# Where a sparse layer's first query projections stand, how memory attention is interleaved, and a final norm taken per token

## The chip, the cores and the metric

The kernel is one program on one core of a Trainium2 chip. The metric is the device time of the whole program in microseconds (us). TensorE (PE) does the matrix products and PEld its weight loads, VectorE is DVE, ScalarE is ACT, GpSimd is POOL, and SyncE (SP) issues most of the DMAs.

## What is computed

The reference is a trunk of two layers over 512 tokens of 1024 features. Each layer adds a mixer and then a gated convolutional FFN to `h`; at the end `h` is normalised. Cut to its frame:

```python
for i in range(DEPTH):                      # DEPTH = 2
    if i == 1:
        shared = shared_kv(h, ...)          # keys and values of the sparse layer
    xn = rmsnorm(h, norm_mix[i])
    mem_kv = rmsnorm(mem, norm_mem[i]) @ w_mem_kv[i]      # 256 memory rows, 4 heads of 64
    if i == 0:                              # gated linear attention
        q, k, v, g, lr, mq = split_cols(xn @ gla_w_in[i], GLA_SIZES)
        main = gla_mixer(...)
    else:                                   # sparse attention, 12 heads of 64, 4 groups
        q, gl, mq = split_cols(xn @ nsa_w_in[0], NSA_SIZES)
        main = nsa_mixer(q, sigmoid(gl), shared, rel_bias)
    mo = mem_attention(mq, mem_kv)          # softmax(mq mem_k) mem_v
    h = h + concatenate([main, mo], -1) @ w_out[i]
    h = h + conv_ffn(rmsnorm(h, norm_ffn[i]), ...)
return rmsnorm(h, final_norm)               # x * rsqrt(mean(x*x) + eps) * gain, per token
```

In `nsa_mixer` every head attends to 31 compressed keys, to selected blocks and to a window, each with a bias by distance.

## The kernel before

**Layout.** Activations stand transposed: `h[k]` (k = 0 to 7) holds 128 features of all 512 tokens. For products in near fp32, `split` makes two fp32r tiles of each: a high half by an ACT copy and the rest by a DVE subtraction (`xh`, `xl`, or `Qh`, `Ql`). A projection onto 128 columns (`projA`) is 8 x 3 = 24 matmuls of 512 columns: wh with xh, wl with xh, wh with xl. `stepsB` makes the values, whose result stands with tokens on the partitions: for each k and each of four token tiles again three matmuls.

**Weights.** `wget` fetches 512 KB by an SP DMA into `wraw` (three buffers), in layer 1 scales it by the gain on POOL, and splits it: ACT makes `wh`, DVE makes `wl`. PSUM has four tags of two banks: `acc`, `sc`, `pt` and `po`.

**Norms.** The squares of `h` are added up into `sqacc` (ACT squares, DVE adds, `sq_step`). `rms_finish` takes the sums over features with four matmuls against a column of ones (L303), makes the reciprocal roots with a POOL `pow` (L306), puts them on a diagonal (DVE, L310), spreads them over the partitions with one matmul of 512 columns (L312) and copies the result to `rb` (ACT).

**Order.** A scheduler sets the order on each engine from the order in which the code is written and from its own estimate of when operands come. In the sparse layer `mm` and `tr` chain TensorE's instructions, so that they stay in written order.

- The start (`gla_layer`): the split of the input, 24 small matmuls for the low-rank gate (`wlr`), then six query and key projections, with `rms_finish` after the first has begun.
- Memory attention (`mem_att`, both layers): twice, for a pair of heads each, it copies the queries to both halves of the partitions (`dup`, four DMAs on SP), splits them, and goes through four tiles of 128 tokens: scores (L395), softmax on DVE and ACT, transposes of the weights (L409), and `fill()`, which emits some steps of the values. At the end of each pair it multiplies the values with the transposed weights (L417).
- Layer 1 after memory attention: `project(0)` (the query projection of the first sparse head pair), `queries(0)` (its `dup` and split, and the `strip` DMAs of the biases), half of `project(1)`, `compressed(0)`, the other half, and `scores(0)`. Then a loop of twelve steps, in which scores, transposes, values and later projections alternate.
- The end (`build`): `rms_finish`, eight products of `h` and the gain on ACT (L1095), eight with `rb` on DVE and POOL (L1098, L1100), and eight DMAs of 256 KB to `outT`, which the host transposes.

## Time and profile before

| | before |
|---|---|
| device time, three runs | 1352.37, 1353.55, 1356.32 us (median 1353.55) |
| the profiled execution | 1353.9 us, with a span of 1352.1 us |
| granted TensorE clock, mean | 0.986 |
| TensorE busy | 1302.7 us, 96% of the span |
| VectorE, ScalarE, GpSimd busy | 840.7, 590.9, 123.3 us |
| DMA | 129.95 MB, 96 GB/s |

The profile is one execution. The span is what it recorded; the 1.8 us by which the execution's own time is longer lies outside. A matmul of 512 columns counts as 0.39 us busy, but the next starts while it drains, so two stand 0.23 us apart at the full clock. An fp32 matmul leaves two records, so counts of those are twice the program's. The granted clock is given as a share of full speed, where 1.00 is 2.4 GHz and 0.50 is 1.2 GHz; a mean between them is a mixture of the two.

### The profile page before, as it was taken

What the parts mean: (1) busy time and instruction counts of PE and PEld (TensorE: products, weight loads), DVE (VectorE), ACT (ScalarE), POOL (GpSimd) and SP (SyncE); (2) the same over time, 40 slices, a digit from 0 to 9 for tenths busy, and PEclk for the clock granted to TensorE, in tenths of its full rate; (3) what the DMA queues carried; (4) which work ended last, traced back from release to release, by engine and by line L of the source; (5) the groups of instructions that cost most, each with busy time, mean ns of one, the idle gap of its engine ahead of it and who ended that gap; (6) DMA issues with size and microseconds to landing.
All of it is one profiled execution on the core that took longest, in us unless ns stands there. A gap on an engine that the chain in (4) does not pass through costs nothing.

```text
span 1352.1 us, 17979 instructions
## 1 busy us (share of the span) xinstructions
PE 1302.7 (96%) x6868; PEld 1052.5 (78%) x6868; DVE 840.7 (62%) x1374; ACT 590.9 (44%) x1060; POOL 123.3 (9%) x102
## 2 busy tenths in 40 slices
PE   7999998999999999999999988999999999999995
PEld 4887776878888888887787666778888888888884
DVE  7556777577777774334466577675577777773223
ACT  6446554444444443223234465665344444442222
POOL 1000000000000000002124243442000000000001
PEclk9999998999999999999999989999999999999997
DMA  6342110323333333333565333211233333333321
GB/s 228 108 136 78 32 33 31 112 81 95 100 101 94 94 97 103 97 94 114 135 186 150 113 88 95 75 47 33 94 94 95 95 102 99 94 94 98 103 65 62
DMA packets 43577, 129.95 MB, mean 96 GB/s; under 512 B 5783, under 2 KB 10039, under 8 KB 43492
## 3 DMA queue, kind: packets, MB, share of 16 engines
q1 hardware_dynamic: 41504, 125.91, 31.6%
q10 hardware_dynamic: 1988, 2.89, 0.7%
q8 instruction: 54, 0.88, 0.3%
q14 instruction: 31, 0.25, 0.1%
HBM read 116.16 MB, written 2.15 MB: 87 GB/s over the span
## 4 chain that ended last, share of the span: by engine, by line
PE 90%; DVE 4%; ACT 2%; DMA 1%; issue 1%; POOL 1%; SPq 0%; DVEq 0%; ACTq 0%; POOLq 0%
PE acc L265 39%; PE acc L709 18%; PE acc L656 6%; PE sc L892 3%; PE po L892 3%; PE acc L284 2%; PE acc L515 2%; PE po L284 2%; PE pt L893 2%; PE acc L892 2%; PE acc L796 2%; PE pt L573 1%; PE sc L824 1%; PE sc L265 1%; PE sc L656 1%
## 5 line engine op out<-in xcount | busy, mean ns | idle before, releaser
L233 DVE TENSOR_TENSOR wl<-wraw,wh 128x1024 fp32r<-128x1024 f32 x196 | 246.6, 1258 | 163.6 <-ACT wh L232 161.3
L232 ACT ACTIVATE wh<-wraw 128x1024 fp32r<-128x1024 f32 x196 | 207.6, 1060 | 290.6 <-PE acc L709 105.9
L265 PE MATMUL acc<-xh,wh 128*128 128x512 f32 x800 | 313.5, 392 | 0.5 <-ACT wh L232 0.5
L265 PE MATMUL acc<-xh,wl 128*128 128x512 f32 x800 | 312.2, 390 | 0.8 <-DVE wl L233 0.8
L265 PE MATMUL acc<-xl,wh 128*128 128x512 f32 x800 | 312.7, 391 | 0.0
L265 PEld LDWEIGHTS acc<-xh,wh 128*128 128x128 f32 x800 | 150.5, 188 | 34.5 <-ACT wh L232 1.9
L265 PEld LDWEIGHTS acc<-xh,wl 128*128 128x128 f32 x800 | 150.6, 188 | 32.6 <-DVE wl L233 1.1
L265 PEld LDWEIGHTS acc<-xl,wh 128*128 128x128 f32 x800 | 150.6, 188 | 31.8 <-issue 0.5
L709 PE MATMUL acc<-ah,wh 128*128 128x512 f32 x352 | 136.9, 389 | 0.0
L709 PE MATMUL acc<-ah,wl 128*128 128x512 f32 x352 | 136.9, 389 | 0.0
L709 PE MATMUL acc<-al,wh 128*128 128x512 f32 x352 | 136.9, 389 | 0.0
L690 DVE TENSOR_TENSOR u<-acc,rb 128x512 f32<-128x512 f32 x88 | 60.6, 688 | 71.2 <-PE acc L265 69.7
L229 POOL TENSOR_TENSOR wraw<-wraw,vec 128x1024 f32<-128x1024 f32 x20 | 38.4, 1925 | 444.9 <-DMA wraw<-in_wp 438.4
L246 ACT ACTIVATE ah<-hc 128x512 fp32r<-128x512 f32 x44 | 27.8, 632 | 116.0 <-DVE hc L697 116.0
L709 PEld LDWEIGHTS acc<-ah,wl 128*128 128x128 f32 x352 | 66.1, 188 | 13.8
L709 PEld LDWEIGHTS acc<-ah,wh 128*128 128x128 f32 x352 | 66.1, 188 | 13.7
L709 PEld LDWEIGHTS acc<-al,wh 128*128 128x128 f32 x352 | 66.1, 188 | 13.7
L692 ACT ACTIVATE hc<-u,vec 128x512 f32<-128x512 f32 x88 | 71.1, 808 | 2.3 <-DVE u L690 1.6
L993 POOL TENSOR_TENSOR P<-P,ssm 128x256 f32<-128x256 f32 (+3 forms) x48 | 62.4, 1321 | 72.3 <-DVE ssm L990 41.1
L693 DVE SCALAR_TENSOR_TENSOR hc<-u,vec,hc 128x511 f32<-128x511 f32 x88 | 65.6, 745 | 5.2 <-ACT hc L692 5.2
L694 DVE SCALAR_TENSOR_TENSOR hc<-u,vec,hc 128x510 f32<-128x510 f32 x88 | 66.1, 751 | 3.1
L696 ACT ACTIVATE hc<-hc 128x512 f32<-128x512 f32 x44 | 27.8, 633 | 83.2 <-DVE hc L694 83.2
(310 smaller groups left out, 2050.0 us busy)
## 6 DMA issues: line engine op xcount, KB each, us to landing
wraw<-in_wp SPq DMA_DIRECT2D x200, 512.0 KB, 3.7
strip<-vecd SPq DMA_DIRECT2D x12, 448.0 KB, 3.6
qd<-qf SPq DMA_DIRECT2D x40, 128.0 KB, 2.3
mt<-in_memT SPq DMA_DIRECT2D x16, 128.0 KB, 3.0
kd<-kf SPq DMA_DIRECT2D x16, 128.0 KB, 2.4
h<-in_xT SPq DMA_DIRECT2D x4, 256.0 KB, 6.4
h<-in_xT ACTq DMA_DIRECT2D x4, 256.0 KB, 6.4
mkd<-mkf SPq DMA_DIRECT2D x16, 64.0 KB, 2.0
```

Of the source, the lines that this page charges most:

```text
L232: nc.scalar.activation(wh, raw, AF.Copy)
L233: nc.vector.tensor_tensor(out=wl, in0=raw, in1=wh.bitcast(F32), op=ALU.subtract)
L265: self.nc.tensor.matmul(ps[:M, :N], a[:, ws], b[:, :N], start=n == 0, stop=n == 23)
L284: nc.tensor.matmul(ps[:, :N], s_, m_, start=k == 0 and n == 0, stop=k == KC - 1 and n == 2)
L656: nc.tensor.matmul(banks[m], a[:, o], b, start=k == 6 and i == 0, stop=k == 5 and i == 2)
L690: nc.vector.tensor_tensor(out=u, in0=ps, in1=rb, op=ALU.mult)
L692: nc.scalar.activation(c, u, AF.Identity, scale=tap(2), bias=tap(3))
L693: nc.vector.scalar_tensor_tensor(out=c[:, 1:], in0=u[:, :S - 1], scalar=tap(1), in1=c[:, 1:], op0=ALU.mult, op1=ALU.add)
L694: nc.vector.scalar_tensor_tensor(out=c[:, 2:], in0=u[:, :S - 2], scalar=tap(0), in1=c[:, 2:], op0=ALU.mult, op1=ALU.add)
L709: nc.tensor.matmul(ps, a[:, o], x, start=n == 0, stop=n == 3 * NJ - 1)
L892: mm = lambda *args, **kw: pe(nc.tensor.matmul(*args, **kw))
L993: nc.gpsimd.tensor_tensor(out=P, in0=P, in1=f[:, i, :].unsqueeze(2).to_broadcast([128, 2, 128 * t + 128]), op=ALU.mult)
```

## The change

There are four parts.

- **Start.** Fourteen fp32 128 x 128 products of a tile of ones stand first on TensorE (their result is not used). The first three weights are split ahead of the squares, and their three projections stand ahead of `rms_finish`. The first takes its eight `wl` products last.
- **Memory attention.** One routine goes through both pairs of heads. Each tile's transposes are issued after the next tile's scores, and the first pair's values product after the second pair's first scores. The values product alternates between the halves of the partitions. `stepsB` yields after each three matmuls, `fill` emits 6 (layer 0) or 4 (layer 1) such steps, and `first` emits 8 steps ahead of the first scores.
- **Sparse layer.** The helpers `project`, `queries`, `pe`, `mm` and `tr` move ahead of memory attention without change but for the pool that they allocate from. `project(0)` becomes what `first` emits; `queries(0)`, the values, and then `project(1)` are the filling. After memory attention come `compressed(0)` and `scores(0)` alone.
- **End.** `last_residual` takes the place of the last norm. The output is written with tokens on the partitions, so the scale of a token is one number per partition.

```diff
+        idle = self.ps("pt")
+        for _ in range(14):
+            nc.tensor.matmul(idle[:, :128], self.ones, self.ones, start=True, stop=True)
...
+        steps = [(k, u, i) for k in range(KC) for u, i in ((wh, 0), (wl, 0), (wh, 1))]
+        if late:
+            steps.sort(key=lambda t: t[1] is wl)
...
         Q[0] = self.stack_q(qfs[0], pool)
+        first()
+        for m in range(2):
+            for qt in range(4):
+                scores(m, qt)
+                if m and not qt:
+                    out(0)
+                if qt == 3 and not m:
+                    Q[1] = self.stack_q(qfs[1], pool)
+                if qt:
+                    turn(m, qt - 1)
+                fill()
+            turn(m, 3)
             fill()
...
+        out(1)
...
+                ps = self.ps("po")
+                self.projA(ps, w, M=16)
+                early = [self.wget(self.W[name][j]) for j, name in ((0, "glak"), (0, "glaq"), (1, "glak"))]
                 for k in range(KC):
                     self.sq_step(k, self.h[k], S)
-                ps = self.ps("po")
-                self.projA(ps, w, M=16)
...
+                qps = [self.ps(tag) for tag in ("acc", "acc", "sc")]
+                for i in range(3):
+                    self.projA(qps[i], early[i], late=i == 0)
                 rc, rb = self.rms_finish(S, "")
...
+                def others():
+
+                    gen = project(0)
+                    for _ in range(8):
+                        yield run(gen, 3)
+                    q = queries(0)
+                    run(q)
+                    for i, _ in enumerate(values()):
+                        if i == 16:
+                            run(q, 3)
+                        yield
+                    gen = project(1)
+                    for _ in range(8):
+                        yield run(gen, 3)
+
+                vs = others()
+                upto = lambda n: lambda: run(vs, n)
+                self.mem_att(qfs, mp, mK, mV, mo, upto(8), upto(4))
...
-                run(project(0), 24)
-                q, c = queries(0), compressed(0)
-                run(q)
-                proj = project(1)
-                run(proj, 12)
-                run(q, 4)
+                c = compressed(0)
                 run(c)
-                run(proj, 12)
                 first = scores(0)
```

The new end, with the old one behind it:

```diff
+    def last_residual(self, m, ps):
+
+        nc, h = self.nc, self.h[m]
+        if m < 7:
+            nc.vector.tensor_tensor(out=h, in0=ps, in1=h, op=ALU.add)
+            self.sq_step(m, h, S)
+            self.hg.append(self.t(self.xp, [128, S], "xh"))
+            nc.scalar.activation(self.hg[m], h, AF.Copy, scale=self.gain(7, m))
+            return
+        sq = self.t(self.tmp, [128, S], "sq", bufs=2)
+        for c in range(2):
+            cs = slice(256 * c, 256 * c + 256)
+            nc.vector.tensor_tensor(out=h[:, cs], in0=ps[:, cs], in1=h[:, cs], op=ALU.add)
+            nc.scalar.activation(sq[:, cs], h[:, cs], AF.Square)
+        self.hg.append(self.t(self.xp, [128, S], "xh"))
+        nc.vector.tensor_scalar_mul(self.hg[m], h, self.gain(7, m))
+        sums = self.ps("pt")
...
+                nc.tensor.transpose(turned[t, half][:, 128 * (k % 4):128 * (k % 4) + 128], self.hg[k][:, tile(t)], self.ident)
+
+        for t in range(4):
+            nc.tensor.matmul(sums[:, t:t + 1], self.sqacc[:, tile(t)], self.ones[:, 0:1], start=True, stop=False)
+            nc.tensor.matmul(sums[:, t:t + 1], sq[:, tile(t)], self.ones[:, 0:1], start=False, stop=True)
+        for t in range(4):
+            turn(t, 0, range(4))
+        rc = self.t(self.small, [128, 4], "rc", bufs=2)
+        nc.vector.tensor_scalar(rc, sums[:, :4], 1.0 / D, EPS, op0=ALU.mult, op1=ALU.add)
+        nc.gpsimd.tensor_tensor(out=rc, in0=rc, in1=self.mhalf[:, :4], op=ALU.pow)
+        for t in range(4):
+            turn(t, 1, (4, 5, 6, 7))
+        for t in range(4):
+            y = self.t(self.wraw, [128, D], "wraw") if t < 3 else self.t(self.wsp, [128, D], "wh")
+            nc.scalar.activation(y[:, :512], turned[t, 0], AF.Copy, scale=rc[:, t:t + 1])
+            nc.vector.tensor_scalar_mul(y[:, 512:], turned[t, 1], rc[:, t:t + 1])
+            nc.sync.dma_start(self.out[128 * t:128 * t + 128, :], y)
...
-            rb = self.rms_finish(S, "")[1]
-            for k in range(KC):
-                nc.scalar.activation(hg[k], self.h[k], AF.Copy, scale=self.gain(7, k))
-            for k in range(KC):
-                if k % 3 == 2:
-                    nc.gpsimd.tensor_tensor(out=hg[k], in0=hg[k], in1=rb, op=ALU.mult)
-                else:
-                    nc.vector.tensor_tensor(out=hg[k], in0=hg[k], in1=rb, op=ALU.mult)
-                (nc.scalar if k % 2 else nc.sync).dma_start(self.out[128 * k:128 * k + 128, :], hg[k])
```

Two places show how TensorE's order moves, and a third SP's. The first is TensorE at the start of layer 1's memory attention. Before, the last product of the second memory query projection (L265) stands directly ahead of the first scores (L395):

```order
L265 MATMUL acc_5934<-xl_5148,wh_5930 128x512
L395 MATMUL sc_5977<-mK_1082_5770,Qh_1114_5964 128x256
L395 MATMUL sc_5977<-mK_1082_5770,Ql_1115_5965 128x256
L284 MATMUL acc_5999<-wh_6006,xh_4508 128x512
L284 MATMUL acc_5999<-wl_6007,xh_4508 128x512
```

Now the 24 products of `project(0)` (L946, the last two of them here) stand there, and the second head's scores (`mK_1085`, `Qh_1118`, `Ql_1119`) one and six rows behind the first head's:

```order
L946 MATMUL acc_6000<-xh_5162,wl_5997 128x512
L946 MATMUL acc_6000<-xl_5163,wh_5996 128x512
L397 MATMUL sc_6027<-mK_1083_5788,Qh_1115_5982 128x256
L397 MATMUL sc_6027<-mK_1083_5788,Ql_1116_5983 128x256
L285 MATMUL acc_6049<-wh_6056,xh_4523 128x512
L397 MATMUL sc_6027<-mK_1085_5794,Qh_1118_5989 128x256
L285 MATMUL acc_6049<-wl_6057,xh_4523 128x512
L285 MATMUL acc_6049<-wh_6056,xl_4524 128x512
L285 MATMUL acc_6050<-wh_6056,xh_4523 128x512
L285 MATMUL acc_6050<-wl_6057,xh_4523 128x512
L397 MATMUL sc_6027<-mK_1085_5794,Ql_1119_5990 128x256
```

Before, the second head's first scores stood 20 rows behind the first head's (a step of 12 values products and other scores between them).

The second place is TensorE from the compressed scores (`kcT`) of `compressed(0)` to the scores of `scores(0)` (`sc` from `K` and `Q`). Before, half of `project(1)` (twelve products into `acc_6376`, of which the first and the last stand here) lay between them:

```order
L892 MATMUL sc_6399<-kcT_5178,qf_6359 128x31
L892 MATMUL sc_6400<-kcT_5178,qf_6359 128x31
L892 MATMUL acc_6376<-xh_4874,wh_6372 128x512
...
L892 MATMUL acc_6376<-xl_5148,wh_6372 128x512
L892 MATMUL sc_6434<-K_951_5173,Qh_1212_6389 128x256
L892 MATMUL sc_6434<-K_951_5173,Ql_1213_6390 128x256
L892 MATMUL sc_6443<-K_951_5173,Qh_1212_6389 128x512
```

Now the scores follow directly, behind the values product of memory attention's second pair (L425):

```order
L425 MATMUL pt_6412<-mPT_1188_6282,mV_5842 64x512
L946 MATMUL sc_6431<-kcT_5193,qf_6025 128x31
L946 MATMUL sc_6432<-kcT_5193,qf_6025 128x31
...
L946 MATMUL sc_6452<-K_952_5188,Qh_1173_6215 128x256
L946 MATMUL sc_6452<-K_952_5188,Ql_1174_6216 128x256
L946 MATMUL sc_6461<-K_952_5188,Qh_1173_6215 128x512
L946 MATMUL sc_6461<-K_952_5188,Ql_1174_6216 128x512
```

From there to the first transposes of the sparse weights, TensorE has the same products in both kernels, but none of `project(1)` now.

The third place is SP's queue around the memory queries' copies (`qd` from `qf`). Before:

```order
L218 DMA wraw_6251<-in_wp 128x1024
L327 DMA qd_5961<-qf_5925 64x512 x2
L218 DMA wraw_6327<-in_wp 128x1024
L327 DMA qd_5968<-qf_5925 64x512 x2
L218 DMA wraw_6369<-in_wp 128x1024
```

Now two bias strips have come between the copies, and one ahead of them:

```order
L974 DMA strip_6047<-vecd_2703 128x896
...
L221 DMA wraw_6205<-in_wp 128x1024
L328 DMA qd_5979<-qf_5943 64x512 x2
L974 DMA strip_6219<-vecd_2703 128x896
L221 DMA wraw_6291<-in_wp 128x1024
L974 DMA strip_6520<-vecd_2703 128x896
L328 DMA qd_5986<-qf_5943 64x512 x2
```

## Rows read from the trace of the kernel before

**Rows 1.** The page: busy time of TensorE, and the chain that ended last

```profile
PE 1302.7 (96%) x6868; PEld 1052.5 (78%) x6868; DVE 840.7 (62%) x1374; ACT 590.9 (44%) x1060; POOL 123.3 (9%) x102
...
PE 90%; DVE 4%; ACT 2%; DMA 1%; issue 1%; POOL 1%; SPq 0%; DVEq 0%; ACTq 0%; POOLq 0%
```

**Rows 2.** Busy time by stretch; behind it clock, DMA share, GB/s

```profile
75.00:115.00 40.00, 39.93 (x208) 31.47 (x206) 20.99 (x38) 20.15 (x43) 0.00 (x0) 1.00 0.39 111
...
726.00:752.00 26.00, 23.42 (x103) 16.78 (x103) 17.95 (x29) 12.58 (x29) 7.69 (x5) 0.93 0.39 109
...
780.00:792.00 12.00, 7.98 (x26) 5.07 (x25) 9.29 (x33) 8.51 (x24) 3.97 (x4) 0.72 0.38 98
792.00:920.00 128.00, 117.70 (x986) 93.78 (x986) 93.97 (x297) 82.19 (x238) 55.47 (x46) 0.99 0.24 66
...
1334.00:1352.20 18.20, 3.10 (x10) 1.47 (x10) 7.79 (x10) 5.84 (x10) 4.44 (x3) 0.60 0.31 115
```

**Rows 3.** Timeline of the start: start us, duration, instruction [idle before]

```profile
10.82 1.41 DVE L250 SCALAR_TENSOR_TENSOR xl<-h,vec,xh 128x512 fp32r<-128x512 f32 x2
...
13.96 0.51 PE L265 MATMUL acc<-xh,wh 128*128 128x512 f32 x1 [0.51 <-ACT wh L232]
...
15.22 0.50 PE L265 MATMUL acc<-xh,wl 128*128 128x512 f32 x1 [0.75 <-DVE wl L233]
...
22.06 1.05 PE L303 MATMUL pt<-ones,sqacc 128*128 128x1 f32 x8 [0.65 <-DVE sqacc L296]
...
26.11 1.12 PE L312 MATMUL pt<-sq,ones 128*128 128x512 f32 x2 [0.38 <-DVE sq L310]
```

**Rows 4.** PE timeline of layer 1's memory attention, 726 to 769

```profile
726.82 0.38 PE L395 MATMUL sc<-mK,Qh 128*128 128x256 f32 x1 [0.71 <-ACT Qh L246]
728.59 0.39 PE L395 MATMUL sc<-mK,Ql 128*128 128x256 f32 x1 [1.39 <-DVE Ql L247]
...
746.20 1.93 PE L417 MATMUL pt<-mPT,mV 128*64 128x512 f32 x4
748.61 1.93 PE L417 MATMUL pt<-mPT,mV 128*64 128x512 f32 x4 [0.48 <-DVE mPT L411]
...
765.56 0.70 PE L409 MATMUL pt<-ident,mP 128*128 128x128 f32 x4 [0.99 <-DVE mP L405]
...
766.66 2.05 PE L417 MATMUL pt<-mPT,mV 128*64 128x512 f32 x8
```

**Rows 5.** PE timeline from the compressed scores to the first turned weights

```profile
776.37 1.08 PE L892 MATMUL sc<-kcT,qf 64*128 64x31 f32 x16
...
787.02 1.03 PE L893 MATMUL pt<-ident,Pc 128*64 128x128 f32 x4 [1.36 <-DVE ssm L987]
...
790.72 0.63 PE L893 MATMUL pt<-ident,P 128*128 128x128 f32 x2
```

**Rows 6.** DMA issues in 722 to 782, count, KB each, median us to landing

```profile
qd<-qf SPq DMA_DIRECT2D x12, 128.0 KB, 2.8
strip<-vecd SPq DMA_DIRECT2D x3, 448.0 KB, 5.4
```

**Rows 7.** Timeline of the end, from the last down-projection matmul

```profile
1333.07 0.39 PE L709 MATMUL acc<-ah,wl 128*128 128x512 f32 x1
...
1333.30 0.39 PE L709 MATMUL acc<-al,wh 128*128 128x512 f32 x1
1333.72 0.69 DVE L318 TENSOR_TENSOR h<-acc,h 128x512 f32<-128x512 f32 x1 [11.96 <-PE acc L709]
...
1336.44 1.02 PE L303 MATMUL pt<-ones,sqacc 128*128 128x1 f32 x8 [2.76 <-DVE sqacc L296]
...
1337.74 1.01 POOL L306 TENSOR_TENSOR rc<-rc,mhalf 128x4 f32<-128x4 f32 x1 [358.32 <-DVE rc L305]
...
1344.11 3.75 SPq L1101 DMA_DIRECT2D outT<-hg  x4
```

**Rows 8.** Bytes in 40 slices of 1340 to 1352, 0.3 us each

```profile
GB/s 0 0 0 0 0 0 0 0 0 0 0 0 0 0 0 0 171 389 382 396 369 41 348 348 376 382 403 362 389 362 382 383 389 389 376 335 21 0 0 0
```

More of the change, by code (lines that the diff above doesn't have):

```diff
@@ L384, in mem_kv, with mem_att, scores @@
         return mK, mV
-    def mem_att(self, l, m, pool, qf, mK, mV, mo, fill=lambda: None):
+    def mem_att(self, qfs, pool, mK, mV, mo, first, fill):
         nc = self.nc
-        Q = self.stack_q(qf, pool)
-        PT = [self.t(pool, [128, 2, S], f"mPT{hh}", bufs=1) for hh in range(2)]
-        for qt in range(4):
+        Q, P, PT = {}, {}, {}
+        def scores(m, qt):
             ts = slice(128 * qt, 128 * qt + 128)
@@ L489, in gla_layer @@
                     vs = values()
-                    fill = lambda: [next(vs, None) for _ in range(2)]
-                    for m in range(2):
-                        self.mem_att(0, m, mp, qfs[m], mK, mV, mo, fill)
+                    upto = lambda n: lambda: [next(vs, None) for _ in range(n)]
+                    self.mem_att(qfs, mp, mK, mV, mo, upto(8), upto(6))
                     for _ in vs:
@@ L710, in ffn, with turn @@
                         n += 1
-                self.residual(m, ps, None, split=not last)
+                if last:
+                    self.last_residual(m, ps)
+                else:
+                    self.residual(m, ps, None)
+    def last_residual(self, m, ps):
[14 more added lines that the diff above has]
+        sums = self.ps("pt")
+        tile = lambda t: slice(128 * t, 128 * t + 128)
+        turned = {}
+        def turn(t, half, ks):
+            if (t, half) not in turned:
+                turned[t, half] = self.ps((("sc", "acc")[half], ("sc", "pt")[half], ("po", "acc")[half], ("po", "pt")[half])[t])
+            for k in ks:
+                nc.tensor.transpose(turned[t, half][:, 128 * (k % 4):128 * (k % 4) + 128], self.hg[k][:, tile(t)], self.ident)
[14 more added lines that the diff above has]
+            nc.sync.dma_start(self.out[128 * t:128 * t + 128, :], y)
@@ L854, in nsa_layer, with pe, project, queries @@
                     pass
+            qp = outer.enter_context(tc.tile_pool(name="nsaq", bufs=1))
+            qfs_, Qs, strips, pos, Ps, PTs = {}, {}, {}, {}, {}, {}
+            steps = [(a, qts) for a in range(6) for qts in ((0, 3), (1, 2))]
+            last = []
+            def pe(ins):
+                if last:
+                    tc.add_manual_dep(ins.ins, last[0].ins.name, mybir.DependencyInfo(mybir.DependencyClass.NoSync, mybir.DependencyReason.DATA),
+                                      reason="order")
+                last[:] = [ins]
+            mm = lambda *args, **kw: pe(nc.tensor.matmul(*args, **kw))
+            tr = lambda *args: pe(nc.tensor.transpose(*args))
+            def project(a):
+                wh, wl = self.wget(self.W["nsaq"][a], GMIX)
+                ps = self.ps("acc")
+                for k in range(KC):
+                    ws = slice(128 * k, 128 * k + 128)
+                    xh, xl = self.x[k]
+                    for i, (u, w) in enumerate(((wh, xh), (wl, xh), (wh, xl))):
+                        mm(ps, u[:, ws], w, start=k + i == 0, stop=k == KC - 1 and i == 2)
+                        if k < KC - 1 or i < 2:
+                            yield
+                qfs_[a] = self.t(qp, [128, S], "qf", bufs=1)
+                nc.vector.scalar_tensor_tensor(out=qfs_[a], in0=ps, scalar=-0.125, in1=rb, op0=ALU.mult, op1=ALU.mult)
+                yield
+            def queries(a):
+                qd = []
+                for hh in range(2):
+                    qd.append(self.t(qp, [128, S], "qd", bufs=2))
+                    self.dup(qd[hh], qfs_[a], 64 * hh)
+                strips[a], Qs[a] = [], []
+                for hh in range(2):
+                    strip = self.t(qp, [128, 896], "strip", bufs=3)
+                    src = self.vecd[a + 6 * hh, :]
+                    nc.sync.dma_start(strip, bass.AP(tensor=src.tensor, offset=src.offset + 1, ap=[[1, 128], [1, 896]]))
+                    strips[a].append(strip)
+                    yield
+                    Qs[a].append([self.t(qp, [128, S], f"Q{c}{hh}", FR, bufs=1) for c in "hl"])
+                    self.split_to(Qs[a][hh][0], Qs[a][hh][1], qd[hh])
+                    yield
+            run = lambda g, n=1: [next(g, None) for _ in range(n)]
             with ExitStack() as ms:
@@ L879, in nsa_layer @@
                     nc.gpsimd.memset(PcT[64:], 0.0)
-                qfs, Qs, strips, pos, Ps, PTs, Pcs = {}, {}, {}, {}, {}, {}, {}
-                steps = [(a, qts) for a in range(6) for qts in ((0, 3), (1, 2))]
-                last = []
-                def pe(ins):
-                    if last:
-                        tc.add_manual_dep(ins.ins, last[0].ins.name, mybir.DependencyInfo(mybir.DependencyClass.NoSync, mybir.DependencyReason.DATA),
-                                          reason="order")
-                    last[:] = [ins]
@@ L1037, in nsa_layer @@
                 main = [None] * 6 + mo
-                run = lambda g, n=1: [next(g, None) for _ in range(n)]
-                run(project(0), 24)
-                q, c = queries(0), compressed(0)
-                run(q)
-                proj = project(1)
-                run(proj, 12)
-                run(q, 4)
+                c = compressed(0)
                 run(c)
-                run(proj, 12)
                 first = scores(0)
```

93 lines of the change are left out of this document (32 added, 61 removed).

## The prediction

> **What bounds the kernel now.** I began with the page: TensorE is busy for 96% of the span, and the chain that ended last is 90% TensorE [rows 1]. The number of products stays as it is, apart from a few small ones. So an edit can gain only where TensorE waits, where it runs at the lower clock, and behind its last product. The busy time by stretch shows where that is [rows 2]. In layer 0's memory attention TensorE is busy 39.93 us of 40.00, so nothing is to be had. In 726 to 752 (layer 1's memory attention) it is 23.42 of 26.00, and the granted clock, 0.93 on average, says that part of it ran at 1.2 GHz. From 780 to 792 it is 7.98 of 12.00 at 0.72. The last 18.2 us hold 3.10 us of TensorE's work. The timelines of these places then give the waits [rows 3 to 5, 7].
>
> **Start, worth about 2.1 us.** The first projection's second product begins at 15.22, after a wait of 0.75 [rows 3]. Products stand 0.23 apart [rows 7], so it goes on as if it had begun at 14.99 and never waited. Now the weights' splits come ahead of the squares and the `wl` products come last, so neither is waited for. What is left is the split of the input: the last two `xl` end at 10.82 + 1.41 = 12.23 [rows 3], and the last gate product follows, so the projection can begin at about 12.5. That is 2.5 gained. Should the gate's products end as now, which is 0.51 ahead of 13.96, it is 1.5. The waits of 0.65 and 0.38 ahead of the norm's two products [rows 3] go as well (1.03), since the sums now come after three projections. A new wait takes their place. From the end of the sums (22.06 + 1.05) to the spreading product at 26.11 are 3.0 us, and only six products (1.4) stand between them now: 1.6 of wait. At the end of the kernel, with nothing beside it, less is possible, so I take 1.4. The sum is 2.5 + 1.0 - 1.4 = 2.1. If the memory rows' work that now stands ahead of the reciprocal on VectorE is late, the wait grows, and I put the low end at 0.5; the high end is 2.8.
>
> The idle products cost nothing in this sum. They leave 28 records of 128 columns. Four transposes of that size took 0.70 with their drain [rows 4], some 0.12 each at the full clock, so 28 take 3.4 us, or 7 at half, from about 1 us on. TensorE has nothing else then, and the gate's 24 products (5.5 at 0.23) need to begin by 7 only if they are to end at 12.5. If the idle ones end at 8 the gate products end at 13.5, which is inside the low end above.
>
> **Layer 0's memory attention, 0.** It is full [rows 2]. A later transpose can hide no wait there, and the larger steps of filling could uncover one. I allow 1 us each way.
>
> **Layer 1's memory attention, worth about 5.6 us.** These are the terms:
>
> - The waits of 0.71 and 1.39 for `Qh` and `Ql` [rows 4] go behind the 24 products of `project(0)` (5.5 us): 2.1.
> - The lower clock follows these two waits. 0.07 of 26 us [rows 2], twice, is 3.6 us at half speed, in which half the work is lost: 1.8.
> - The first pair's values product ran in two halves one after the other, with 0.48 between, 746.20 to 750.54. The second pair's same eight records took 2.05 [rows 4]. With the halves alternating, both should take that: 4.34 - 2.05 = 2.3. If the alternation does not make the difference, 0.5.
> - The transposes' wait of 0.99 [rows 4] is covered by the next tile's scores: 1.0.
> - Against it, the second head's scores now stand one product behind the first head's. Their queries' copy must wait until `Ql` has read the one buffer (728.6, as before), and takes 2.8 us to land [rows 6] and a split of about 0.6: 732.0. TensorE gets there at about 726.1 + 5.5 + 0.5 = 732.1. But two strips and a weight now stand between the two copies on SP, and a strip of 448 KB took 5.4 us to land [rows 6]. So the wait lies between 0 and 2.6 us. I take 0.8, near the low end, since the strips can be issued before the buffer is free. What is queued behind these scores on TensorE is all the filling.
> - For new short waits (transposes for their softmax, evictions) I take another 0.8.
>
> The sum is 2.1 + 1.8 + 2.3 + 1.0 - 0.8 - 0.8 = 5.6; 2.5 to 7.2 with the ends.
>
> **Compressed scores and first scores, 0.** From 776.37 to the first turned weights at 790.72 are 14.35 us [rows 5]. The twelve products of `project(1)` in it (2.7) move elsewhere, which leaves 11.6 that is a chain of scores, softmax on VectorE and ScalarE, and transposes; the 1.36 ahead of 787.02 [rows 5] is one of its waits. The queries are now split earlier, which shortens it, and VectorE no longer has a query projection's eviction in between. But TensorE now has nothing to do in the waits, and the lower clock (0.72 over 12 us is 6.7 us at half [rows 2]) may last longer. I take 0, with 1.5 either way.
>
> **End, worth about 4.8 us.** The last product ends at R = 1333.30 + 0.39 = 1333.69 [rows 7]. Before, the first output DMA was issued at 1344.11, R + 10.4, after the sums, the power, the diagonal, the spreading, its copy and the multiplication. Now: two half additions (0.69 for a whole one [rows 7]) and the second half's square bring the sums' start to R + 1.3. They are eight products of one column, 16 records where eight took 1.02 [rows 7], so they end at R + 3.4. From there to the end of the power were 1.3 us (1337.46 to 1338.75 [rows 7]): R + 4.7. One pass over 512 columns each on ScalarE and VectorE, 0.7, and the first DMA goes at R + 5.5 or R + 5.6. Of the 32 transposes (0.12 each, 3.8 us), twelve stand between the sums and the rest ends at about R + 6, ahead of the later scalings. After its first DMA the old kernel took 1352.1 - 1344.1 = 8.0 us, for 2.1 MB at some 380 GB/s [rows 8]. With the same 8.0 the end comes at R + 13.6 and not at R + 18.4: 4.8. The gain multiplications that moved into the down projection stand on ScalarE beside a VectorE that was idle 11.96 us there [rows 7] and a TensorE that did not wait; uncovered, each would cost a pass of 512 columns, 0.7. The low end is 3.2 (transposes at half speed), the high end 5.5.
>
> **Sum.** 2.1 + 0 + 5.6 + 0 + 4.8 = 12.5. The profiled execution took 1353.9, which makes 1341.4. The median of the runs is 0.35 lower, so I forecast 1341.
>
> **The rivals.**
>
> *Given back in layer 1.* The strips are late (2.6 of wait, not 0.8), and the bare chain costs the 1.5 above and another 4 us at half speed behind it (2.0). That loses 5.3: about 1346.5. For it: SP's order, and that products which filled a stretch of waits are gone. Against it: the chain itself gets no new step.
>
> *Transposes at half speed.* The last 32 transposes run without a matmul beside them, after a pause of TensorE that was 2.76 us before the sums [rows 7], in a stretch with a mean clock of 0.60 [rows 2]. They then cost 0.24 each, and the later 16 delay the last DMAs by 1 to 2 us: 1343. Against it, four transposes took 0.70 in the midst of products at the full clock [rows 4]. The Trainium skill, "TensorE: Matmul & The Clock Gate", Part 4 on PE-mode transposes, says that transposes do not count as TensorE activity and the full clock does not engage for them; by that rule this rival is certain, and the forecast would be 1343. The rows do not decide it.
>
> *One queue for the output.* All four DMAs now go by SP, where two engines issued before. If SP's queue alone moves half of the 380 GB/s, 2.1 MB take 11 us and not 5.5, and the end's gain is gone: 1346.5. Against it stands only that the weights come by SP's queue alone throughout and TensorE hardly waits for them; no row shows that queue with this much asked of it at once. The Trainium skill, "DMA: Bandwidth & Descriptors", on issuing engines, says that the queues share the same 16 DMA engines and that issuing from several saves only issue time; by it this rival falls away.
>
> *The other side: slower.* The stand of TensorE behind `compressed(0)` leaves the clock at 1.2 GHz into the sparse loop. Each us there costs half a us. To end 4 us above 1353.55 it must eat 12.5 + 4, so 33 us more at half speed. Against it: at present the clock is 0.72 in 780 to 792 and 0.99 from 792 to 920 [rows 2], so it came back at once. From 60 us of it the time would be 1371.
>
> *No difference.* If the interleaving of both attentions gains nothing, and the start only its low end, the end alone remains: 1353.55 - 4.8 - 0.5, about 1348; with the end's low value too, 1350.
>
> **How the numbers follow.** The forecast with its terms near the values taken gets 0.55, given back in layer 1 0.17, half-speed transposes 0.14, one queue 0.04, no difference 0.06, slower 0.04. The forecast's own range is 1337.5 to 1344. Taking in the first two rivals and the bounds of the terms gives 1336.5 to 1347.5. A measurement of this kernel can tell a change of 0.3%, or 4 us, from none. Faster than 1349.5 are the forecast and the first three rivals, nearly all: 0.89. Same gets 0.07, slower 0.04.
>
> **What would show it.** Right: the first `glak` product at 12.5 to 13; no wait over 0.5 us ahead of L397 but one of at most 1 us at `Qh` of the second head; both L425 groups near 2.05; about 11 to 12 us from the compressed scores to the first turned weights; the first output DMA 5.6 us after the last down-projection product, the end 13.6 after it. Wrong: a low clock at 732 to 740, or beyond 795; transposes of the end 0.2 apart; landings of the output spread over more than 8 us; a wait over 2.5 ahead of the spreading product at the start.

## The result and the profile after

The changed kernel took 1341.25 us in the median of four runs (1337.29 to 1341.56), and the kernel before beside it 1353.66: a ratio of 0.9899, with a 95% interval from 0.9875 to 0.9923. In a second measurement six runs gave 1342.19 against 1351.25, 0.9927 (0.9902 to 0.9952). The forecast was 1341, with 1336.5 to 1347.5 as its range.

The profiled execution after was the fastest of the four, 1337.29 us, and so 4 us under the median. A second profile of the same kernel (called again below) took 1344.87. The two are read side by side here, since they differ by more than some of the terms.

These are the busy times by stretch, cut at the instructions that begin and end the stages of the prediction: from the first key projection to the last memory query product of layer 0, layer 0's memory attention, layer 1 from its memory values to the compressed scores, from there to the first turned weights, from there to the last down-projection product, and the end. The columns are the stretch, its length, busy time and count of PE, PEld, DVE, ACT and POOL, the granted clock, DMA share and GB/s. Before:

```profile
13.96:80.35 66.39, 63.59 (x311) 51.98 (x312) 44.27 (x67) 34.32 (x54) 4.76 (x3) 0.97 0.48 140
80.35:127.60 47.25, 47.17 (x274) 37.72 (x273) 25.41 (x53) 25.81 (x60) 0.00 (x0) 1.00 0.30 87
...
708.47:776.37 67.90, 63.73 (x311) 48.63 (x309) 42.88 (x67) 30.97 (x68) 20.54 (x13) 0.97 0.46 129
776.37:790.72 14.35, 10.33 (x47) 7.02 (x47) 9.92 (x32) 7.31 (x20) 4.35 (x4) 0.79 0.53 133
790.72:1333.69 542.97, 531.95 (x2929) 436.52 (x2927) 334.71 (x605) 242.30 (x443) 61.54 (x52) 1.00 0.28 82
1333.69:1352.10 18.41, 3.10 (x10) 1.47 (x10) 8.07 (x10) 6.12 (x10) 4.44 (x3) 0.60 0.31 114
```

After, in its first profile:

```profile
12.97:76.72 63.75, 61.49 (x312) 50.90 (x312) 44.66 (x68) 35.26 (x57) 4.52 (x3) 1.00 0.48 147
76.72:123.03 46.31, 45.64 (x274) 37.89 (x272) 25.71 (x53) 26.60 (x61) 0.00 (x0) 1.00 0.33 95
...
703.67:769.21 65.54, 62.25 (x323) 49.67 (x321) 40.12 (x69) 31.99 (x70) 21.20 (x11) 1.00 0.51 150
769.21:780.11 10.90, 7.30 (x37) 4.84 (x36) 7.89 (x30) 5.52 (x17) 3.67 (x6) 0.69 0.37 96
780.11:1322.69 542.58, 531.45 (x2932) 436.75 (x2930) 334.91 (x607) 246.27 (x452) 61.37 (x51) 1.00 0.28 82
1322.69:1335.50 12.81, 5.27 (x48) 4.93 (x47) 4.13 (x8) 3.14 (x6) 1.01 (x1) 0.89 0.41 164
```

And again, the same kernel in another execution:

```profile
12.89:77.58 64.69, 63.00 (x312) 51.95 (x312) 45.43 (x69) 36.42 (x57) 4.47 (x3) 0.97 0.49 151
77.58:123.18 45.60, 45.48 (x274) 37.85 (x272) 25.28 (x53) 26.15 (x60) 0.00 (x0) 1.00 0.32 88
...
704.46:771.85 67.39, 62.02 (x323) 49.65 (x321) 40.50 (x68) 32.36 (x71) 23.63 (x12) 1.00 0.50 147
771.85:782.80 10.95, 7.19 (x37) 4.61 (x36) 7.93 (x31) 5.84 (x18) 3.67 (x6) 0.77 0.37 96
782.80:1330.27 547.47, 536.37 (x2932) 440.51 (x2930) 334.65 (x605) 246.44 (x450) 61.37 (x51) 0.99 0.27 81
1330.27:1343.10 12.83, 5.27 (x48) 4.93 (x47) 4.13 (x8) 3.14 (x6) 1.01 (x1) 0.92 0.41 163
```

The gains by stage follow from the lengths. For the start it is the place where the stage ends that counts (80.35, then 76.72 and 77.58). Twelve products of `project(1)`, 2.7 us, are taken out of the fifth stage of before and put to layer 1's, where they now are. The 127.60 to 708.47 of before, 580.87 us, took 580.64 and 581.28.

| stage | forecast | first profile | again |
|---|---|---|---|
| start | 2.1 | 3.6 | 2.8 |
| layer 0's memory attention | 0 | 0.9 | 1.6 |
| layer 1's memory attention | 5.6 | 5.1 | 3.2 |
| compressed and first scores | 0 | 0.7 | 0.7 |
| sparse loop to last product | 0 | 0.4 | -4.5 |
| end | 4.8 | 5.6 | 5.6 |
| between the layers' attentions | 0 | 0.2 | -0.4 |
| sum | 12.5 | 16.6 | 9.0 |

The stretch from the first turned weights to the last product holds the same 2932 records of TensorE in both executions of one kernel, yet they were busy 531.45 and 536.37 us. That is the clock, 1.00 against 0.99 on average, and the length goes with it: what is left beside the busy time is 11.13 and 11.10 us, so the waits are the same in sum. In pieces of 12 us, the first profile's clock is under 1.00 in one (0.86 from 852.11), and that of again in five (the lowest are 0.72 from 830.80 and 0.86 from 806.80).

Now the places that answer to [rows 3 to 5, 7, 8]. The start, on TensorE's timeline after:

```profile
1.05 5.17 PE L211 MATMUL pt<-ones 128*128 128x128 f32 x28 [1.05 <-DVE ones L208]
...
12.97 0.40 PE L267 MATMUL acc<-xh,wh 128*128 128x512 f32 x1
...
32.52 1.10 PE L313 MATMUL pt<-sq,ones 128*128 128x512 f32 x2 [0.74 <-DVE sq L311]
```

The idle products fill 1.05 to 6.2, the first key projection begins at 12.97 (before, in effect, at 14.99), and the one wait of the norm is 0.74 [rows 3]. Layer 1's memory attention, and behind it the compressed scores:

```profile
723.69 0.93 DVE L250 TENSOR_TENSOR Ql<-qd,Qh 128x512 fp32r<-128x512 f32 x1 [1.73 <-ACT Qh L249]
...
724.64 1.11 SPq L328 DMA_DIRECT2D qd<-qf  x2
...
726.71 0.28 PE L397 MATMUL sc<-mK,Ql 128*128 128x256 f32 x1
...
728.72 0.39 PE L397 MATMUL sc<-mK,Qh 128*128 128x256 f32 x1 [1.50 <-ACT Qh L249]
...
748.00 1.94 PE L425 MATMUL pt<-mPT,mV 128*64 128x512 f32 x8
...
767.34 1.94 PE L425 MATMUL pt<-mPT,mV 128*64 128x512 f32 x8
769.21 1.08 PE L946 MATMUL sc<-kcT,qf 64*128 64x31 f32 x16
...
776.77 1.03 PE L947 MATMUL pt<-ident,Pc 128*64 128x128 f32 x4 [2.10 <-ACT P L1080]
...
780.11 0.38 PE L947 MATMUL pt<-ident,P 128*128 128x128 f32 x2
```

The waits ahead of the first head's scores are gone, and one of 1.50 stands ahead of the second head's, for `Qh`. The copy for it is issued at 724.64, as soon as the first head's `Ql` has read the one buffer (724.62). Both values products take 1.94 us, where the first took 4.34 with its wait [rows 4]. From 769.21 to 780.11 TensorE waits 2.10 in one piece for the softmax. The end:

```profile
1322.30 0.39 PE L741 MATMUL acc<-al,wh 128*128 128x512 f32 x1
...
1326.05 0.60 PE L772 MATMUL acc<-ident,xh 128*128 128x128 f32 x4
...
1327.86 1.65 SPq L788 DMA_DIRECT2D out<-wraw  x3
```

and the bytes in 40 slices of 1320 to 1335.5:

```profile
GB/s 0 0 0 0 0 0 0 0 0 0 0 0 0 0 0 0 0 0 0 0 0 0 243 412 391 412 391 402 412 370 423 423 402 423 402 307 0 0 0 0
```

The last product ends at 1322.69, the first output DMA is issued 5.2 us after it (10.4 before), four transposes take 0.60 (the granted clock is 1.00 from 1322.69 to 1328.00, while they run), and one queue moves 370 to 423 GB/s, where two moved some 380 [rows 8].

### The profile page after: what moved, and what is told of

It reads as the page before. It is cut to its first block, busy times and chain, and to the rows that moved or that the text cites. A ratio compares the mean times of both kernels' runs of the same rounds, so it can differ in the third digit from the quotient of the medians.

```text
span 1335.5 us, 18101 instructions
## 1 busy us (share of the span) xinstructions
PE 1299.7 (97%) x6934; PEld 1058.8 (79%) x6934; DVE 831.7 (62%) x1372; ACT 591.1 (44%) x1063; POOL 119.8 (9%) x100
```

## The experiments

All times are medians beside the kernel before on the same chip, which took 1350.6 to 1351.6 there. A single profile is read for its waits, and the whole time only with its interval.

**The same kernel again.** No edit.

> The changed kernel, unaltered. Its first profile (1337.3 us) lies 4 us under the median of its runs (1341.25). Clock theory: the usual run has some 8 us more at 1.2 GHz (which costs 4 us) at a place where that profile ran at full speed, and the waits are the same. Rival: a wait for a DMA is longer in the usual run, and the clock is the same. Time 1341.

Measured: 1342.19 (six runs, 1339.48 to 1345.01). The profile is the third table above. It shows both. In the sparse loop the waits are the same and the clock is lower (4.9 us longer). In layer 1's memory attention the wait ahead of the second head's scores is 3.10 and not 1.50, and another, of 0.54 in the first profile, is 1.23.

```profile
731.46 0.39 PE L397 MATMUL sc<-mK,Qh 128*128 128x256 f32 x1 [3.10 <-ACT Qh L249]
```

Here too the copy was issued as soon as the buffer had been read (`Ql` ends at 725.51, the copy goes at 725.54), but `Qh` could begin only at 730.78, 5.2 us after that and not 3.4 as in the first profile. So these two profiles differ by the clock first, and by the landing of this copy second.

**Without the idle products.** The three lines of the idle products are left out.

> The changed kernel without the fourteen idle products. Theory: they only bring the full clock from 9.8 to 4.8 us, and the gate's products are paced by the split of the input anyhow, so the first key projection begins 0.5 us later: 1341.8. Rival: they also decide that the clock does not fall at the four gate products near 43 us, as it did before the change; then another 1.7 us: 1343.5.

Measured: 1345.04 (twelve runs), 0.9952 (0.9936 to 0.9969), against 0.9927 (0.9902 to 0.9952) with them: about 3 us worse, nearer the rival. The intervals overlap a little, so the profile has to carry the reading, and in it the clock fell in another place than the rival said. VectorE and TensorE around the norm in this kernel:

```profile
29.96 0.95 PE L301 MATMUL pt<-ones,sqacc 128*128 128x1 f32 x8
...
32.58 0.48 DVE L250 SCALAR_TENSOR_TENSOR ml<-mt,vec,mh 128x256 fp32r<-128x256 f32 x1
32.98 0.15 DVE L303 TENSOR_SCALAR rc<-pt 128x4 f32<-128x4 f32 x1
...
35.09 1.22 PE L310 MATMUL pt<-sq,ones 128*128 128x512 f32 x1 [2.68 <-DVE sq L308]
```

The sums end at 30.91, but the reciprocal (`rc`, the DVE row at 32.98) stands behind rows of the memory tiles, the last at 32.58, that the scheduler put ahead of it, and the spreading product waits 2.68, where it waited 0.74. The clock then falls: from 32 to 45 us it is 0.74. The last query product of layer 0 ends the stage at 81.85, 5.1 us later than in the first profile after and 4.3 later than again. Of that, 0.7 is the later first projection (13.63 against 12.97) and 1.9 the wait; the rest lies in the stretch at the lower clock. From the first projection (13.63) to 32.40 the clock is 1.00 in this kernel too, although its gate products had begun at the lower one. So the later rise of the clock accounts for the 0.7, and the other loss follows the wait.

**Eight idle products.** With eight, the order that the scheduler makes around the norm is that of fourteen.

```diff
-        for _ in range(14):
+        for _ in range(8):
```

> The changed kernel with eight idle products and not fourteen. The written order on VectorE around the norm is then that of fourteen (without any, one more row of the memory tiles stands ahead of the reciprocal). Theory: most of what the idle products gave at the start was this order, which cut the wait ahead of the spreading product from 2.7 to 0.7 us and kept the clock up behind it; then eight give the same 0.7, the first key projection begins at 13 to 13.6, and the gate bias's products at 40.6 to 41.2: 1341.5. Rival: it was the clock's earlier rise, and with eight the clock rises later and the start loses 3 us or more: 1344.

Measured: 1340.44 (six runs), 0.9924 (0.9906 to 0.9943). Its start on TensorE:

```profile
1.05 3.72 PE L211 MATMUL pt<-ones 128*128 128x128 f32 x16 [1.05 <-DVE ones L208]
...
31.58 1.10 PE L313 MATMUL pt<-sq,ones 128*128 128x512 f32 x2 [0.74 <-DVE sq L311]
```

The wait is 0.74, as with fourteen. The gate's products start 0.22 to 0.25 apart from the first on, where the input is there, so the clock was full by then, as with fourteen; without any idle products they start up to 0.43 apart until 10.33. So this run alone does not part the two causes (order, clock); the profile without idle products does, as said above. The first projection begins at 12.02, earlier than the 13 to 13.6 expected, and the stage ends at 76.74, as with fourteen (76.72). So six of the fourteen were not needed.

**The queries back behind memory attention.** The old sequence of `project(0)`, `queries(0)`, half of `project(1)`, `compressed(0)`, the other half; the new memory attention is kept, filled with values alone.

```diff
-                vs = others()
+                vs = values()
...
-                c = compressed(0)
+                run(project(0), 24)
+                q, c = queries(0), compressed(0)
+                run(q)
+                proj = project(1)
+                run(proj, 12)
+                run(q, 4)
                 run(c)
+                run(proj, 12)
```

> The changed kernel with the sparse queries' projections and their copies back behind memory attention, as before the change; memory attention keeps its new order, with eight steps of values ahead of its first scores. Theory: the place of the projections is most of the 5 us that layer 1's memory attention gained, since without them the filling runs out in the second pair of heads, and the waits for the first sparse queries come back: 3 us more, 1344. Rival: the later transposes and the values ahead do it alone: within 1 us of 1341.

Measured: 1340.63 (four runs), 0.9921 (0.9894 to 0.9948), not parted from the changed kernel. The 3 us that the theory asked for did not come, and the rival's forecast did. Its waits on TensorE in layer 1's memory attention:

```profile
725.51 0.50 PE L285 MATMUL acc<-wh,xh 128*128 128x512 f32 x1 [2.53 <-DVE qf L351]
...
731.84 0.39 PE L397 MATMUL sc<-mK,Qh 128*128 128x256 f32 x1 [1.50 <-ACT Qh L249]
...
763.87 0.41 PE L416 MATMUL pt<-ident,mP 128*128 128x128 f32 x2 [1.52 <-DVE mP L407]
```

There are 2.53 (the values' first bank is still held by the memory query), 1.50 (the second head's queries, as in the changed kernel), and 1.52 at the end of the second pair, where the filling has run out. In return the stretch from the compressed scores to the first turned weights takes 11.73 with twelve products in it, against 10.90 without: those twelve cost 0.8 there, not 2.7. From the memory values (703.78) to the first turned weights (782.03) are 78.25 us; the changed kernel took 76.44 and 78.34.

**The old end.** `last_residual` is replaced by the old norm, multiplication and eight DMAs.

> The changed kernel with the old final norm. Theory: the whole of what the end lost from the last product to the end of the span (18.4 to 12.8) comes back, 5.6 us: 1346.9. Rival: the clock or the one queue gives part of it back in the usual run, so that only about 3 us come: 1344.

Measured: 1347.95 (ten runs), 0.9983 (0.9963 to 1.0003), which is 5.8 us above the changed kernel. The stretch of the end in its profile:

```profile
1333.03:1351.40 18.37, 3.10 (x10) 1.47 (x10) 8.07 (x10) 6.12 (x10) 4.44 (x3) 0.60 0.31 114
```

18.37 us, as before [rows 2], against 12.81. The theory holds in full.

**The halves in the old order.** In the values product of memory attention, the loop over halves goes outside again.

```diff
-            for kt in range(2):
-                for hh in range(2):
+            for hh in range(2):
+                for kt in range(2):
```

> The changed kernel with memory attention's values product in the old order, one half of the partitions after the other. Theory: alternating the halves is what lets two of these products run side by side, so each of the four groups takes 4 us and not 1.94, and 8 us are lost: 1349. Rival: they overlapped before the change too wherever both halves were ready (one of two groups in layer 1 took 2.05), because the scheduler had put the halves together; then the groups stay near 2 and the time at 1341.

Measured: 1344.01 (seven runs), 0.9939 (0.9918 to 0.9961), which the intervals do not part from the changed kernel. The first pair's product in layer 1, in this kernel:

```profile
751.22 1.94 PE L425 MATMUL pt<-mPT,mV 128*64 128x512 f32 x8
```

All four groups take 1.94 or 1.95. The order in the code does nothing; the rival holds.

**A second buffer for the copied memory queries.**

```diff
-            qd = self.t(pool, [128, S], "qd", bufs=1)
+            qd = self.t(pool, [128, S], "qd", bufs=2)
```

> The changed kernel with two buffers, not one, for the copied memory queries, so that the second head's copy need not wait until the first head's split has read the buffer, and stands on SP's queue ahead of the strips. Theory: this copy's wait for its buffer, behind two strips, is what TensorE waits 1.5 to 3.6 us for ahead of the second head's first scores; the wait goes, and from the memory values' evictions to the first turned sparse weights it takes 74.9 us, where the changed kernel's two profiles took 76.4 and 78.3. Time 1339. Rival: the copies are bound by the DMA engines, not by the buffer, and the wait stays above 1 us: 1341 to 1342.

Measured: 1340.57 (six runs), 0.9918 (0.9897 to 0.9939), not parted from the changed kernel. The wait ahead of the second head's scores is gone, so it was the one buffer that held this copy. Another has come, of 3.92, ahead of the transposes:

```profile
738.11 2.95 DVE L236 TENSOR_TENSOR wl<-wraw,wh 128x1024 fp32r<-128x1024 f32 x1
...
741.17 0.62 DVE L407 TENSOR_SCALAR mP<-mP,msm 128x256 f32<-128x256 f32 x2
...
741.66 0.68 PE L416 MATMUL pt<-ident,mP 128*128 128x128 f32 x4 [3.92 <-DVE mP L407]
```

The last multiplication of that tile's softmax (`mP`, DVE at 741.17) stands on VectorE behind a weight's split that took 2.95 us (1.20 in the changed kernel at 739.02; why it took longer stays open). From the memory values to the first turned weights it took 79.40 us (703.50 to 782.90), where 74.9 had been expected. The wait moved from the copy to VectorE's queue.

**The strips ahead of memory attention.** Three strips are fetched before the memory keys' work.

```diff
...
+            loaded = {}
+            for ah in ((0, 0), (0, 1), (1, 0)):
+                loaded[ah] = load(*ah)
...
-                    strips[a].append(strip)
+                    strips[a].append(loaded.pop((a, hh), None) or load(a, hh))
```

> The changed kernel with the first three bias strips fetched ahead of memory attention, so that none stands on SP's queue between the two copies of the memory queries; the copies keep their one buffer and the engines their order. Theory: the strips' 1.3 MB, and not the buffer, make the second head's copy land late; TensorE's wait ahead of the second head's first scores falls from 1.5 to 3.6 us to under 1, without the wait for the transposes that came with a second buffer (3.9 us): 1339.5. Rival: the weights on the same queue delay the copy as much, and the wait stays above 1.5: 1341.5.

Measured: 1345.41 (twelve runs), 0.9960 (0.9946 to 0.9975): some 3 us slower than the changed kernel. The intervals overlap a little, but that of the kernel with eight idle products, on the same chip, ends at 0.9943. The profile is that of the slowest run (1351.53) and is read for its order alone:

```profile
725.00 0.50 PE L946 MATMUL acc<-xh,wh 128*128 128x512 f32 x1 [0.94 <-ACT wh L235]
...
726.82 4.90 SPq L221 DMA_DIRECT2D wraw<-in_wp  x3
...
726.85 0.50 PE L946 MATMUL acc<-xh,wl 128*128 128x512 f32 x1 [1.34 <-DVE wl L236]
...
731.28 2.38 DVE L250 TENSOR_TENSOR Ql<-qd,Qh 128x512 fp32r<-128x512 f32 x1
...
733.69 6.24 SPq L328 DMA_DIRECT2D qd<-qf  x8
...
733.72 0.38 PE L397 MATMUL sc<-mK,Ql 128*128 128x256 f32 x1 [1.27 <-DVE Ql L250]
...
738.01 0.39 PE L397 MATMUL sc<-mK,Qh 128*128 128x256 f32 x1 [1.59 <-ACT Qh L249]
```

No strip stands between the copies now, and the second one is still late, so the theory falls. Nor is it the weights on SP's queue, as the rival had it: SP had issued its three by 731.72. The copy is issued at 733.69, when the first head's `Ql` has read the buffer (731.28 + 2.38 = 733.66). That split stands on VectorE behind splits of weights. TensorE waits 1.27 for it and 1.59 for the second head's `Qh`. The strips also went ahead of `project(0)`'s weight on SP, and TensorE waits 0.94 and 1.34 for that.

**Half of `project(1)` between the first scores.**

```diff
-                    gen = project(1)
-                    for _ in range(8):
+                    gen = proj1
+                    for _ in range(4):
                         yield run(gen, 3)
...
                     run(first)
                     if i in (1, 3):
                         run(c)
+                    run(proj1, 2)
```

> The changed kernel with half of project(1) emitted two products at a time between the scores of scores(0), and not ahead of compressed(0). Theory: the chain of scores, softmax and transposes sets that stretch, so twelve products in it are nearly free; the compressed scores to the first turned weights take 11 to 12 us with them, as without, and up to 2.7 us are gained: 1340. Rival: memory attention's second pair misses them and waits for its own softmax instead, or the products delay the scores: 1342 or more.

Measured: 1338.72 (four runs, 1337.56 to 1340.10), 0.9905 (0.9879 to 0.9931): lower than the theory's 1340, but not parted from the changed kernel. From the memory values to the first turned weights it took 75.63 us in its profile, against 76.44 and 78.34 for the same products. The theory's 11 to 12 us cannot be read off, since in this kernel the compressed scores begin ahead of memory attention's last values product.

**With it, the second buffer; or the earlier strips.**

> Both edits, the second buffer and the products between the first scores. If each removes its own wait, the stretch from the memory values' evictions to the first turned weights is 4 us shorter than in the changed kernel's first profile (72.5, where that took 76.4): 1337. If they share a wait, 74 to 75, and 1339.

Measured: 1340.44 (six runs), 0.9911 (0.9883 to 0.9939).

> The earlier strips together with half of project(1) between the first scores. If both waits go: 1337.5, from the memory values' evictions to the first turned weights 74 us. If the earlier products make the softmax of memory attention's last tiles late instead: 1339 to 1340.

Measured: 1345.20 (eight runs), 0.9959 (0.9944 to 0.9974). Neither adds to it: the same stretch took 75.79 us with the second buffer, where 72.5 to 75 were expected, and 80.40 with the earlier strips, where 74 was. With the second buffer TensorE waits 3.13 for the transposes, and with the earlier strips 1.34 and 1.53 for `project(0)`'s weight and the second head's queries.

**With it, eight idle products.**

> Half of project(1) between the first scores, and eight idle products: the two edits that looked best or equal. Theory: the products between the scores are worth 1 to 2 us beyond the changed kernel in its usual runs (1340.6 to 1342.2), and eight idle products do what fourteen do: 1339. Rival: the shorter time of the first of the two (1338.7 in four runs) was the clock's luck, and the time is 1341.

Measured: 1337.88 (six runs, 1336.27 to 1341.29), 0.9902 (0.9878 to 0.9926). The same three stretches of layer 1 in its profile:

```profile
705.14:765.99 60.85, 56.92 (x299) 46.62 (x297) 40.84 (x66) 30.26 (x68) 22.31 (x11) 1.00 0.54 153
765.99:779.18 13.19, 11.00 (x59) 7.59 (x59) 7.75 (x33) 5.97 (x19) 3.68 (x6) 1.00 0.14 40
779.18:1324.11 544.93, 533.18 (x2932) 437.61 (x2930) 336.45 (x607) 247.09 (x451) 61.36 (x51) 0.99 0.28 84
```

The middle stretch is not the same work as in the changed kernel: the compressed scores begin ahead of memory attention's last transposes and values product, so these lie in the 13.19 us too, beside the twelve products. What can be compared is the whole, from the memory values to the first turned weights: 74.04 us, against 76.44 and 78.34, for the same products. From the compressed scores on the clock is 1.00 here (as in the kernel with fourteen idle products and this edit), where it was 0.69 and 0.77 in the changed kernel. The time in microseconds is the lowest of all versions, but its ratio of 0.9902 is not parted from the changed kernel's 0.9899 and 0.9927. So the rival, that the shorter time was the clock's luck, is not excluded by the times.

## Why the prediction was right, point by point

**The sum** was 12.5, and the medians moved by 12.4 in one measurement and 9.1 in the other. The two profiles give 16.6 and 9.0. So the sum was right as a middle. That it came so near is in part luck: most terms came out larger than forecast, and layer 1's second head and, in one execution, the clock of the sparse loop took back what they gave.

**Start, 2.1 forecast, 2.8 where the clock did as before.** Again has the same lower clock as before (0.97 from the first projection to the end of the stage), and ends 2.8 earlier; the first profile ran that stretch at 1.00 and ends 3.6 earlier. The wait ahead of the spreading product was 0.74, where I had taken 1.4. The first projection began at 12.97, not 12.5. For the idle products I saw only that they cost nothing. What I left out is that they keep the reciprocal ahead of the memory rows on VectorE: without them about 3 us are lost. The risk that I named for the low end, the memory rows ahead of the reciprocal on VectorE, is what the kernel without the idle products shows, 2.68 of wait.

**Layer 0's memory attention, 0 forecast, 0.9 to 1.6.** It was full, and I concluded that nothing was to be had. But a full TensorE can do the same 274 records faster: it was busy 47.17 us before, and 45.64 and 45.48 after. Values products of 512 columns start 0.23 apart, those of 256 columns 0.12. The steps from a values product into transposes were longer: the eight of before took 0.94 more than these distances. Now five of the eight groups of transposes come straight from scores, at 0.12, and the other three took 0.36 more. The steps out of the transposes, 3.32 before and 2.99 now, gave another 0.33. So these changes of kind account for 0.9 of the 1.5 to 1.7; the rest stays open. That the first profile gained 0.9 and again 1.6 lies in a wait: TensorE waits 0.56 at 78.57 in the first profile for an eviction (`qf`), and not in again.

**Layer 1's memory attention, 5.6 forecast, 5.1 and 3.2.** The waits for the first head went as forecast. The clock's 1.8 went too: its mean is 1.00 in this stretch in both profiles, and was 0.97 before. The wait for the second head's copy was mis-sized: 0.8 taken, 1.5 and 3.1 measured, up to 2.6 allowed. I put its risk in SP's order, and that is not where it lay: in both profiles the copy was issued as soon as the buffer was free, and the second buffer removed the wait. Two sizes were off. The copy landed 3.4 and 5.2 us after its issue, where 2.8 was taken; why it took 5.2 once stays open. And the buffer came free 2.6 and 2.9 us ahead of TensorE, where I had reckoned with 3.5 (728.6 to 732.1). The values product's 2.3 came (4.34 to 1.94), but not by "the halves alternating": in the old order they take 1.94 too. What is left as its cause is that the product is issued after the next scores, when both halves' transposes are done; no run put that back. And the place of the queries, which gives the change its name, is worth nothing that was measured: the kernel with the queries back takes the same time. So the new memory attention did the work of this term. That is by elimination, since no run has its old order in the changed kernel.

**Compressed and first scores, 0 forecast, 0.7.** Within the bounds. The bare chain wastes time: in the kernel with the queries back, the same stretch with twelve products more in it took only 0.8 us more. The clock was 0.69 and 0.77 in the bare stretch, and 0.86 there.

**End, 4.8 forecast, 5.6.** The first DMA went 5.2 us after the last product, not 5.6, and the rest took 7.6 and not 8.0. The old end put back costs 5.8.

**The rivals.** Given back in layer 1 came in part: again lost 2.4 of the 5.6, though by the landing of a copy and not by SP's order. Transposes at half speed did not come: four took 0.60 at the end, and 0.60 or 0.68 in memory attention (1.03 at 776.77, in the stretch with a mean clock of 0.69). The rule of the Trainium skill ("TensorE: Matmul & The Clock Gate", Part 4, PE-mode transposes), that the full clock does not engage for transposes, is not borne out by these rows: the end's transposes began right behind products, and the clock was 1.00 until the last of them (1322.69 to 1328.00). What a longer run of transposes alone would do, no run here shows. One queue for the output was as fast as two, which agrees with the Trainium skill, "DMA: Bandwidth & Descriptors", on issuing engines: both feed the same 16 DMA engines. The slower case did not come. In again the clock is lower in the sparse loop, and 4.5 us are lost, but only a small part of that stands right behind the bare chain (0.93 in the first 12 us); the larger falls come later, from 806.80 on. It goes with the execution and not with the kernel, since the first profile of the same kernel does not have it.

## What to carry to other kernels

Before a transfer is moved on a queue, it is worth reading what the transfer waited for. Here it was a buffer: moving the strips did not help, and a second buffer removed that wait and brought another on VectorE. Filling a waiting stretch with other work (twelve products among the first scores) shortened it in two profiles, by 0.8 to 4.3 us, but the whole times do not part it from the changed kernel. Where one scheduler orders all engines, a few instructions that compute nothing can change what stands ahead of a short, critical one on another engine; the order around such an instruction is to be read, not assumed. Before a term of 2 us is believed, the same kernel should be profiled twice.

## What the runs showed that I had not expected

The clock alone makes two executions of one kernel differ by 5 us in one stretch. In the sparse loop TensorE was busy 531.4 us for 2932 records in three kernels' profiles (542.5 to 542.6 us long), 533.4 in the one with eight idle products (544.54), and 536.4 again (547.47); the time beside it was 11.1 us in all of these. So a median over a few runs carries a part of this, and a gain of 2 us was to be seen only in the lengths of single stretches.
